# Residual stream with channels on the partitions, and 128-row scores with queries fetched from DRAM, in a two-layer decoder trunk

## Chip, cores and metric

The kernel runs on one core of a Trainium2 chip. Time is device time of one launch, in microseconds. Several executions of each kernel are timed; one more is profiled, and all rows below come from that one.

## What is computed

Two decoder layers on x of 512 tokens by 1024 channels, all in float32. Each layer is an RMS norm, one input projection split into parts, two attention branches with gates, an output projection added to x, and then a per-layer embedding (PLE). Cut to what matters here:

```python
for i in range(2):
    h = rms_norm(x, norm_gain[i])
    y = even_layer(h) if i == 0 else odd_layer(h)     # @ w_in, attention, gates, @ w_out
    x = x + y
    gate = sigmoid(rms_norm(x, ple_norm_gain[i]) @ w_ple_gate[i])
    x = x + (p[i] @ w_ple_proj[i]) * gate
# odd layer: C (8 heads, dilated keys) and D (4 heads, two softmax maps each), head size 64
s = einsum('bqhd,bshd->bhqs', q, k) * scale           # q, k: normed, rotated
```

A scores sum thus runs over 64 numbers. The kernel keeps precision by splitting each operand of a big matmul into a high and a low part in the fast float form ("fp32r"), and adding products of parts.

## The kernel before

**Data.** T = 512 tokens make NT = 4 tiles of P = 128; D = 1024 channels make NK = 8. The residual stream X is kept as two halves of the channels, X[half][:, t, :], tokens on the partitions. AT holds the normed input (without its scale) transposed: channels on the partitions, as high and low parts, `AT[:, part, k, tokens]`. `slot` is a ring of eight large SBUF buffers (L308), `raw` of four weight pieces of 128x512 and `w2` of eight split ones.

**Projections.** `proj_tok` (L406) computes tokens x columns: for each token tile t and channel block k three matmuls (high x high, high x low, low x high) with AT as the stationary operand and the weights moving, 12 matmuls for each weight piece over four tiles. Order "kt" goes through the pieces with four PSUM banks open; "tok" finishes tile after tile. `proj_gate` (L441) has the weights stationary and needs the tokens' norm scale along the free axis: `scale_rows` (L494) writes the scales to DRAM and reads them back to all partitions.

**Norms.** `norm` (L510) runs three times: before PLE of either layer, and before layer 1. For each of 4 tiles and 2 halves `turn` (L502) transposes four 128x128 blocks of X on TensorE into an `sk` bank and copies high and low parts into AT; `norm_scale` (L483) sums squares along the free axis with ScalarE and takes the power -1/2 on GpSimd. Layer 0 begins with a transposed copy of x from the host, so its input norm has no transposes.

**Scores of C and D.** `head_evac` (L571) norms, rotates and transposes queries and keys and `put_heads` (L557) stores them with 64 channels of an even head on partitions 0 to 63 and of an odd head on 64 to 127 (for D the two maps). `score_pairs` (L632) issues, for the three products of parts, a matmul on the lower 64 rows and one on the upper 64, in turn, each half with a bank of its own. Layer 0 does it differently already: `put_stacked` (L561) copies keys by DMA so that one tile holds high parts on one half of the partitions and low parts on the other, and `scores` (L624) runs two 128-row matmuls.

**Ends.** `out_half` (L729) adds the output projection to X (`add_x`, L702); `ple` (L744) evacuates with tanh of bank times the tokens' scale, two more steps on VectorE and a store.

**Order.** Nothing is issued as it is written. `Program` (L80) records every call, prices it, and `order` (L226) plays a list schedule: each engine takes the ready call with the lowest place, the place being the program's minus a lead from the table LEADS (one number for each use of a part such as "mm", "ev", "att", "w"). `issue` then emits all calls, so every instruction of the profile carries one line, L278; groups have to be read by their tiles. Each engine runs its own list strictly in order. In names, `mm` are projection banks, `sk` score banks, `tk` transpose banks, `ob` output banks.

Of the kernel before, what the change touches and what calls it, by code (L numbers as in the profile page):

```python
# [21 lines left out]
P = 128  # L22
# [9 lines left out]
    "att": (-392, -476, -265, 55, 575, -382, 44, 15, -6, -149, -341, -446, -4, -57, 63, -14, 2, 2, -287, 388, 0, 0,  # L32
# [7 lines left out]
    "idx": (-5, -2, 0),  # L40
    "mm": (15, 0, 153, 0, 10, -336, -84, 2, 8, 4, 0, -30, 30, -5, 88, -12, -304, 0, 41, 13, 136, -25, 206, -141, -135,
         -6, -996, -1930, -2303, -10383),
    "norm": (-3, -2, 0, -170, 60, -38, 0, -13, 142, 15, 0, -227, 0, -49, 15, -1, 0, 0, -396, -7, 21, 0, 0, -1844),
    "rows": (0, 898),
    "ss": (-64, 0, 0, 340, 576, 4, -39, 1269, 0, 0, -74, 119, 196, 55, 333, 112, -4, 45, -250, -182, 70, 0, 0, 1, 14,
         -119, 0, 74, 0, 1, 0, -88),
    "tab": (279, 13, -4, 0, -137, -2),
    "top": (193, -101, -908, -1349, 180, 58, -8, -21, -2, 3, -1659, -1846),
    "w": (-57, 169, 413, -21, 0, -44, -172, 0, 3, 0, -2, 1, -44, 74, -2, -20, -89, 234, 3, 68, -363, 0, 0, -80, -19,
         0, -19, 0, -854, -1336),  # L50
    "x": (2, 0),
    "y": (825, 483, 0, -2, -20, 0, 0, -16, 32, 4, 0, 202, 1, -123, -517, -335),
    None: 62,
# [4 lines left out]
SWITCH = 200  # L58
WHOLE = frozenset(range(512))
PR = 8  # L60
QB = 2
# [18 lines left out]
class Program:  # L80
# [18 lines left out]
    def __init__(self, tc):  # L99
        self.tc = tc  # L100
        for e in self.ENGINES:
            setattr(self, e, _Engine(self, e))
        self.calls, self.cost, self.after, self.rank = [], [], [], []
        self.lead, self.parts = LEADS.get(None, 0), {}
        self.touched, self.users, self.rings, self.bytes, self.groups = {}, {}, {}, {}, {}
        self.mode, self.joined, self.place, self.extra = {}, None, 0, {}
# [23 lines left out]
    def _price(self, engine, method, reads, writes):  # L130
# [22 lines left out]
        return 218 / 128 * n  # L153

    @contextmanager
    def together(self):

        self.joined = []
        yield
        i, = set(self.joined)  # L160
        self.cost[i] /= 2
        self.joined = None

    def add(self, engine, method, args, kw):
        if self.joined:
            i = self.joined[0]
            self.calls[i][1].append((method, args, kw))
        else:
            i = len(self.calls)
            self.calls.append((engine, [(method, args, kw)]))  # L170
            self.rank.append((self.place - self.lead, i))
            self.cost.append(0)
            self.after.append(set())
        self.place += 1
        if self.joined is not None:
            self.joined.append(i)
# [4 lines left out]
        if engine == "tensor":  # L181
            self.mode[i] = reads[0].ap[0][1], writes[0].ap[0][1]
# [43 lines left out]
    def order(self):  # L226
# [17 lines left out]
        dma, mode = 0.0, None  # L244
# [4 lines left out]
        while len(out) < n:  # L249
# [6 lines left out]
            if i in self.mode:  # L256
                t += SWITCH * (mode not in (None, self.mode[i]))
                mode = self.mode[i]
# [23 lines left out]
def tile_trunk(ctx: ExitStack, tc: tile.TileContext, a: dict, out: bass.AP):  # L282
# [123 lines left out]
    def proj_tok(pieces_n, evac, tiles=range(NT), order="kt", act=None, swap=0, cut=False, first=False):  # L406
# [5 lines left out]
        def mms(t, i, c0=0, c1=n, passes=range(3)):  # L412
            kt, w2 = pieces[i]
            for c in passes:
                xa, wa = PASSES[c]
                nc.tensor.matmul(banks[t][:, c0:c1], act[kt ^ (4 * swap)][:, xa, t * P:(t + 1) * P], w2[:, wa, c0:c1],
                                 start=(i == 0 and c == 0), stop=(i == last and c == 2))
        if order == "kt":
# [10 lines left out]
            for t in tiles:  # L429
                evacuate(evac, t, banks[t])  # L430
        else:
            for t in tiles:
                halves = ((0, 256), (256, 512)) if cut and t == NT - 1 else ((0, n),)
                for c0, c1 in halves:
                    banks[t] = mm_bank()
                    for i in range(last + 1):
                        mms(t, i, c0, c1)
                    evacuate(evac, t, banks[t], *((c0, c1) if cut else ()))

    @nc.part("mm")  # L440
    def proj_gate(pieces_n, y0, done, rsb):  # L441
# [3 lines left out]
        for i, (kt, w2) in enumerate(pieces):  # L445
            for m in range(4):
                for c, (xa, wa) in enumerate(PASSES):
                    nc.tensor.matmul(banks[m], w2[:, wa, m * P:(m + 1) * P], AT[:, xa, kt, :],
# [34 lines left out]
    def norm_scale(t, rs, times=1.0):  # L483
# [5 lines left out]
        if times != 1.0:  # L489
            nc.vector.tensor_scalar(out=e, in0=e, scalar1=times ** -2, scalar2=None, op0=ALU.mult)  # L490
# [11 lines left out]
    def turn(t, half, to):  # L502
        b = s_bank()
        for i in range(4):
            nc.tensor.transpose(b[:, i * P:(i + 1) * P], X[half][:, t, i * P:(i + 1) * P], ident)
        hs = slice(to * 4, to * 4 + 4)
        bv = b.rearrange("p (k n) -> p k n", k=4)
        hilo(AT[:, 0, hs, t * P:(t + 1) * P], AT[:, 1, hs, t * P:(t + 1) * P], bv)

    def norm(times=1.0, swap=0):  # L510
        rs = sb.tile([P, NT], F32, name=uid("rsn"), tag="rsn", bufs=2)
        for t in range(NT):
            for half in range(2):
                turn(t, half, half ^ swap)
            norm_scale(t, rs, times)
        return rs
# [44 lines left out]
    def put_stacked(dst, t, bank):  # L561
# [3 lines left out]
        for j, d in enumerate(dst):  # L565
# [3 lines left out]
            nc.sync.dma_start(out=d[other].bitcast(F32), in_=lo[own].bitcast(F32))  # L569

# [61 lines left out]
    def score_pairs(qT, kT, wants):  # L632

        banks = [s_bank(), s_bank()]
        found, o = [], 0
# [4 lines left out]
        found.reverse()  # L640
# [489 lines left out]
```

## Time and profile before

| | us |
|---|---|
| three runs | 676.76 median, 676.32 to 677.66 |
| profiled execution | 677.39 |
| its span, first to last instruction | 675.6 |
| TensorE busy | 668.0 (99%), 3494 matmul instructions |
| VectorE busy | 513.7 (76%) |
| ScalarE busy | 415.4 (61%) |
| GpSimd busy | 68.7 (10%) |
| DMA | 74.23 MB, 35% of 16 engines' time |

The page's timeline of 40 slices shows TensorE at nine tenths or more in every slice but the first and the last, and VectorE there from the third slice to the thirteenth (attention of layer 0) and again around the attention of C.

A matmul's busy time runs from its start to its modelled end, and the next one starts before that end. What one costs an engine that never waits is therefore the distance between starts. In the chain of waits a run of matmuls stands with its length from the first start to the start of what follows, which gives that distance directly.

### The profile page before, as it was taken

How to read it: one execution, taken by the hardware profiler on the slowest of the kernel's cores; microseconds unless marked ns; L12 is line 12 of the kernel's file. 1: busy time of each engine (PE TensorE's matmuls, PEld its weight loads, DVE VectorE, ACT ScalarE, POOL GpSimd, SP SyncE). 2: the span in 40 equal slices, each digit the busy share in tenths (PEclk: the TensorE clock that was granted, in tenths of full speed). 3: DMA queues.
4: the chain of work that ended last, by engine and by line, in shares of the span. 5: the costliest groups of instructions: out<-in, count | busy, mean ns of one | idle time of the engine just before them, and what ended most of it. 6: DMA issues, size and time to landing. Idle time of an engine off the chain costs nothing.

```text
span 675.6 us, 10378 instructions
## 1 busy us (share of the span) xinstructions
PE 668.0 (99%) x3494; PEld 543.9 (81%) x3494; DVE 513.7 (76%) x1225; ACT 415.4 (61%) x957; POOL 68.7 (10%) x55
## 2 busy tenths in 40 slices
PE   8999999999999999999999999999999999999997
PEld 5888888888988888887778877777887777888886
DVE  6699999999999646464795298989869698655443
ACT  6765678999889725355554365766637476564341
POOL 0120132000100000000230040003031000100100
PEclk9999999999999999999999999999999999999999
DMA  9855146653131521253353322123213034132222
GB/s 333 299 144 153 63 126 168 183 148 141 48 111 49 185 79 54 71 183 101 87 156 99 94 62 79 48 63 94 86 40 97 29 114 136 48 111 63 93 79 78
DMA packets 49621, 74.23 MB, mean 110 GB/s; under 512 B 5920, under 2 KB 18592, under 8 KB 49312
## 3 DMA queue, kind: packets, MB, share of 16 engines
q1 hardware_dynamic: 49424, 73.56, 35.3%
q8 instruction: 27, 0.44, 0.3%
q14 instruction: 26, 0.21, 0.1%
q10 hardware_dynamic: 144, 0.02, 0.0%
HBM read 61.49 MB, written 6.30 MB: 100 GB/s over the span
## 4 chain that ended last, share of the span: by engine, by line
PE 92%; DMA 3%; DVE 2%; ACT 1%; issue 1%; SPq 0%; DVEq 0%; ACTq 0%
PE mm L278 70%; PE sk L278 8%; PE ob L278 7%; PE tk L278 6%; DMA raw<-in_w_in_odd_dram 2%; DMA slot<-in_xT_dram 1%; DVE t L278 1%; DMA raw<-in_w_out_odd_dram 1%; DVE w L278 1%; ACT w L278 0%; DVE AT L278 0%; ACT t L278 0%; DVE slot L278 0%; SPq L278 0%; DVE tiny L278 0%
## 5 line engine op out<-in xcount | busy, mean ns | idle before, releaser
L278 PE MATMUL mm<-w,AT 128*128 128x512 f32 (+2 forms) x1728 | 433.6, 397 | 1.2 <-ACT w L278 0.6
L278 PEld LDWEIGHTS mm<-w,AT 128*128 128x128 f32 x1728 | 313.4, 188 | 69.6 <-issue 1.6
L278 PE MATMUL mm<-AT,w 128*128 128x512 f32 x384 | 104.9, 404 | 0.0
L278 ACT ACTIVATE w<-raw,gains 128x512 fp32r<-128x512 f32 x96 | 67.7, 722 | 58.8 <-PE mm L278 51.5
L278 DVE SCALAR_TENSOR_TENSOR w<-raw,gains,w 128x512 fp32r<-128x512 f32 x96 | 69.9, 746 | 39.1 <-ACT w L278 38.7
L278 POOL TENSOR_TENSOR tiny<-tiny,mhalf 128x8 f32<-128x8 f32 (+1 forms) x32 | 56.9, 1780 | 351.2 <-DVE tiny L278 351.2
L278 PEld LDWEIGHTS mm<-AT,w 128*128 128x128 f32 x384 | 68.6, 189 | 12.9 <-issue 1.1
L278 ACT ACTIVATE pr<-pr,nm 128x256 f32<-128x256 f32 (+3 forms) x128 | 68.6, 539 | 11.6 <-DVE nm L278 11.3
L278 PE MATMUL sk<-slot,slot 128*128 128x256 f32 (+7 forms) x368 | 64.6, 330 | 0.0
L278 DVE TENSOR_TENSOR w<-raw,w 128x512 fp32r<-128x512 f32 x80 | 53.8, 682 | 14.0 <-ACT w L278 13.6
L278 ACT CAST w<-raw 128x512 fp32r<-128x512 f32 x79 | 47.6, 620 | 22.2 <-PE mm L278 13.4
L278 PEld LDWEIGHTS sk<-slot,slot 64*128 64x128 f32 (+1 forms) x368 | 43.9, 187 | 12.0 <-issue 3.8
L278 PE MATMUL tk<-ident,pr 128*128 128x128 f32 x256 | 43.7, 275 | 0.0
L278 DVE SCALAR_TENSOR_TENSOR t<-t,slot 128x512 f32<-128x512 f32 (+1 forms) x17 | 11.2, 659 | 35.0 <-ACT t L278 35.0
L278 PEld LDWEIGHTS ob<-pt,Ve 128*128 128x128 f32 x272 | 35.1, 191 | 2.7 <-ACT pt L278 1.2
L278 PE MATMUL ob<-pt,Ve 128*128 128x128 f32 x272 | 37.2, 276 | 0.0
L278 PEld LDWEIGHTS tk<-ident,pr 128*128 128x128 f32 x256 | 31.2, 141 | 7.0 <-ACT pt L278 1.5
L278 ACT ACTIVATE t<-mm,rsn 128x512 f32<-128x512 f32 (+1 forms) x17 | 11.0, 662 | 40.0 <-PE mm L278 40.0
L278 DVE TENSOR_TENSOR t<-raww,tab 128x512 f32<-128x512 f32 x48 | 32.4, 684 | 4.0 <-ACT raww L278 3.9
L278 DVE CUSTOM_DVE_ANT_0 pr<-sk,cpack 128x128 f32<-128x128 f32 (+3 forms) x72 | 31.1, 461 | 5.6 <-PE sk L278 5.5
L278 ACT COPY pt<-tk 128x512 f32<-128x512 f32 (+3 forms) x56 | 27.4, 489 | 12.1 <-PE tk L278 8.6
L278 POOL TENSOR_TENSOR rsn<-tiny,mhalf 128x1 f32<-128x1 f32 x16 | 11.3, 710 | 215.6 <-DVE tiny L278 215.5
(100 smaller groups left out, 797.1 us busy)
## 6 DMA issues: line engine op xcount, KB each, us to landing
raw<-in_w_in_odd_dram SPq DMA_DIRECT2D x64, 256.0 KB, 2.8
raw<-in_w_in_even_dram SPq DMA_DIRECT2D x36, 256.0 KB, 3.0
raw<-in_w_ple_gate_dram SPq DMA_DIRECT2D x32, 256.0 KB, 2.6
slot<-in_x_dram SPq DMA_DIRECT2D x16, 256.0 KB, 6.6
raw<-in_w_out_even_dram SPq DMA_DIRECT2D x16, 256.0 KB, 2.8
raw<-in_w_out_odd_dram SPq DMA_DIRECT2D x16, 256.0 KB, 2.6
slot<-qh SPq DMA_DIRECT2D x22, 128.0 KB, 2.4
slot<-ql SPq DMA_DIRECT2D x22, 128.0 KB, 2.5
```

The lines of the kernel that those rows point to most:

```text
L278: getattr(getattr(nc, engine), method)(*args, **kw)
```

## The change

X is kept with channels on the partitions throughout: X[c][:, t, :] is now channel block 4c + t with all 512 tokens. The projections that write X (`out_half`, `ple`, `ple_products`) are flipped: weights stationary, AT moving. A norm needs no transposes: `split_x` copies a block's high and low parts into AT, `add_squares` sums squares over blocks, `column_scales` sums over partitions with one-column matmuls against -1/2, and `scale_rows` makes the row form by TensorE transposes and not through DRAM. PLE multiplies by that row before tanh. Input and output go through the host transposed. A third order of a projection, "mix", opens four banks for the first four pieces and then finishes tile by tile; with `swap` two neighbouring projections use the two halves of AT the other way round.

Keys of C and D are stacked as in layer 0 (`put_stacked`). Queries go to DRAM as high and low parts (`put_far`), and before each score group `fetch` brings a head pair's block of 128 queries to both halves of the partitions, into one of three SBUF homes used in turn (they held layer 0's values and index scores). A group is then four 128-row matmuls for each head pair and query block. The price of a change of matmul form is gone from the planner, and LEADS is a new table.

```diff
-    def score_pairs(qT, kT, wants):
+    def fetch(far, p, qb):
+        n = fetched[0] = fetched[0] + 1
+        q = sb.tile([P, 2, 2, P], F32R, name=uid("q"), tag=HOMES[n % len(HOMES)], bufs=1)
+        for u in range(2):
+            nc.sync.dma_start(out=q[64 * u:64 * u + 64].bitcast(F32),
+                              in_=far[qb][:, :, p, :].rearrange("c (j d) n -> d c j n", j=2))
+        return q
+
+    def score_pairs(far, kT, wants):
         banks = [s_bank(), s_bank()]
...
         for p, qb in reversed(wants):
             n = (qb + 1) * P
-            found.append((p, qb, o, n))
+            q = fetch(far, p, qb)
+            for j, bank in enumerate(banks):
+                for c in range(2):
+                    nc.tensor.matmul(bank[:, o:o + n], q[:, c, j, :], kT[j][:, p, :n], start=c == 0, stop=c == 1)
...
-        with nc.together():
-            for p, qb, o, n in found[::-1]:
-                for c, (qa, ka) in enumerate(PASSES):
-                    for j, bank in enumerate(banks):
-                        rows = slice(64 * j, 64 * j + 64)
-                        nc.tensor.matmul(bank[:, o:o + n], qT[qa][rows, p, qb * P:(qb + 1) * P],
-                                         kT[ka][rows, p, :n], start=c == 0, stop=c == 2)
+    def put_far(dst, t, bank):
+        hi, lo = [sb.tile([P, 4, P], F32R, name=uid(x), tag=x, bufs=QB) for x in ("qh", "ql")]
+        hilo(hi, lo, bank.rearrange("p (k n) -> p k n", k=4))
+        home = dram.tile([2, P, 4, P], F32, name=uid("far"), tag=uid("far"), bufs=1)
+        for c, part in enumerate((hi, lo)):
+            nc.sync.dma_start(out=home[c], in_=part.bitcast(F32))
+        dst[t] = home
...
     def scale_rows(rs):
+        b = t_bank()
+        for t in range(NT):
+            nc.tensor.transpose(b[:, t * P:(t + 1) * P], rs[:, t:t + 1].to_broadcast([P, P]), ident)
         rows = sb.tile([P, T], F32, name=uid("rows"), tag="rows", bufs=1)
-        line = dram.tile([NT, P], F32, name=uid("line"), tag=uid("line"), bufs=1)
-        nc.sync.dma_start(out=line.rearrange("t p -> p t"), in_=rs)
-        nc.sync.dma_start(out=rows, in_=line.rearrange("t p -> (t p)").partition_broadcast(P))
+        nc.scalar.copy(out=rows, in_=b)
         return rows
...
-    def turn(t, half, to):
-        b = s_bank()
-        for i in range(4):
-            nc.tensor.transpose(b[:, i * P:(i + 1) * P], X[half][:, t, i * P:(i + 1) * P], ident)
...
+    def split_x(k, to):
+        hilo(AT[:, 0, to, :], AT[:, 1, to, :], X[k // 4][:, k % 4, :])
+    def add_squares(acc, k):
+        sq = acc if k == 0 else tmp()
+        nc.scalar.activation(out=sq, in_=X[k // 4][:, k % 4, :], func=AF.Square, scale=1.0 / 32.0)
+        if k:
+            nc.vector.tensor_tensor(out=acc, in0=acc, in1=sq, op=ALU.add)
+    def column_scales(acc, times):
+        b = t_bank()
+        for t in range(NT):
+            nc.tensor.matmul(b[:, t:t + 1], acc[:, t * P:(t + 1) * P], mhalf[:, :1], start=True, stop=True)
...
     def norm(times=1.0, swap=0):
+        acc = sb.tile([P, T], F32, name=uid("qh"), tag="qh", bufs=QB)
+        for k in range(NK):
+            split_x(k, k ^ (4 * swap))
+            add_squares(acc, k)
+        rs = column_scales(acc, times)
+        return rs, scale_rows(rs)
...
+        elif order == "mix":
+            early = [t for t in tiles if not (cut and t == NT - 1)]
+            for t in early:
+                banks[t] = mm_bank()
+            for i in range(4):
+                for t in early:
+                    mms(t, i)
+            for t in early:
+                for i in range(4, last + 1):
+                    mms(t, i)
+                evacuate(evac, t, banks[t])
...
-                nc.scalar.activation(out=th, in_=bank[:, c0:c1], func=AF.Tanh, scale=rs[:, t:t + 1])
+                nc.vector.tensor_tensor(out=th, in0=bank[:, c0:c1], in1=rows[:, c0:c1], op=ALU.mult)
+                nc.scalar.activation(out=th, in_=th, func=AF.Tanh)
```

Three places show how the order moves. TensorE at the end of layer 0's output projection, where PLE's norm is taken; before (`slot_784` and `slot_785` are the halves of X, `mm_831` to `mm_833` output projection banks):

```order
L278 MATMUL mm_831<-w_829,AT 128x512 x3
L278 MATMUL sk_835<-ident,slot_784 128x128
L278 MATMUL mm_832<-w_823,AT 128x512
L278 MATMUL sk_835<-ident,slot_784 128x128
L278 MATMUL mm_832<-w_823,AT 128x512
L278 MATMUL sk_835<-ident,slot_784 128x128
L278 MATMUL mm_832<-w_823,AT 128x512
L278 MATMUL sk_835<-ident,slot_784 128x128
L278 MATMUL mm_832<-w_825,AT 128x512 x2
L278 MATMUL sk_836<-ident,slot_785 128x128
```

TensorE at PLE's first projection in the change, where the same norm ends (`qh_833` holds the squares, `rsn_843` the scales, `mm_863` to `mm_866` PLE's banks):

```order
L259 MATMUL tk_841<-mhalf,qh_833 128x1
L259 MATMUL mm_866<-AT,w_854 128x512 x2
L259 MATMUL mm_863<-AT,w_856 128x512 x3
L259 MATMUL mm_863<-AT,w_858 128x512 x3
L259 MATMUL mm_863<-AT,w_860 128x512 x3
L259 MATMUL mm_863<-AT,w_862 128x512 x3
L259 MATMUL tk_844<-ident,rsn_843 128x128 x3
L259 MATMUL mm_864<-AT,w_856 128x512
L259 MATMUL tk_844<-ident,rsn_843 128x128
L259 MATMUL mm_864<-AT,w_856 128x512 x2
```

The transposes of X between the output projection's matmuls are gone; PLE's first bank is finished before the four transposes of the scales stand in PE's list.

TensorE at the first score group of C; before (`slot_941`, `slot_942` are the keys' parts, `slot_1038`, `slot_1039` the queries'; six rows of 128 columns for the other query block follow):

```order
L278 MATMUL mm_1153<-AT,w_1083 128x512
L278 MATMUL sk_1095<-slot_941,slot_1038 128x256
L278 MATMUL sk_1096<-slot_941,slot_1038 128x256
L278 MATMUL sk_1095<-slot_942,slot_1038 128x256
L278 MATMUL sk_1096<-slot_942,slot_1038 128x256
L278 MATMUL sk_1095<-slot_941,slot_1039 128x256
L278 MATMUL sk_1096<-slot_941,slot_1039 128x256
```

The same engine in the change, from the third query block of the first pair to the first of the second (ahead of these rows stand the matmuls of query 1089 and two projection matmuls):

```order
L259 MATMUL mm_1245<-w_1172,AT 128x512 x2
L259 MATMUL sk_1092<-slot_916,q_1094 128x384 x2
L259 MATMUL sk_1093<-slot_917,q_1094 128x384 x2
L259 MATMUL mm_1151<-AT,w_1082 128x512
L259 MATMUL mm_1245<-w_1172,AT 128x512
L259 MATMUL mm_1152<-AT,w_1082 128x512
L259 MATMUL sk_1097<-slot_916,q_1099 128x512 x2
L259 MATMUL sk_1098<-slot_917,q_1099 128x512 x2
L259 MATMUL mm_1246<-w_1172,AT 128x512
L259 MATMUL mm_1152<-AT,w_1082 128x512
L259 MATMUL mm_1246<-w_1172,AT 128x512
L259 MATMUL sk_1119<-slot_916,q_1121 128x256 x2
```

A group is four matmuls of full height, and groups stand closer. Query 1121 takes the home of query 1089.

SyncE's queue (SP), which issues nearly all DMAs, over the same stretch in the change (`far` are the queries in DRAM, `q` the fetched blocks, `raw` weight pieces):

```order
L259 DMA far_1033<-ql_1032 128x512
L259 DMA raw_1293<-in_w_in_odd_dram 128x512
L259 DMA q_1089<-far_1033 64x4x128 x2
L259 DMA q_1121<-far_1044 64x4x128 x2
L259 DMA q_1122<-far_1033 64x4x128 x2
L259 DMA q_1127<-far_1055 64x4x128 x2
L259 DMA q_1132<-far_1066 64x4x128 x2
L259 DMA q_1221<-far_1055 64x4x128 x2
L259 DMA q_1215<-far_1044 64x4x128 x2
L259 DMA raw_1295<-in_w_in_odd_dram 128x512
```

Fetches now stand between the weight loads of the next projections. Over the whole program SP has 399 DMA issues and had 291; PE's list has 3198 matmuls and had 3330 (a plain-float one of them becomes two instructions in the profile).

## Rows read from the trace of the kernel before

**Rows 1.** Page, part 1: engine, busy us, share, instructions.
```profile
PE 668.0 (99%) x3494; PEld 543.9 (81%) x3494; DVE 513.7 (76%) x1225; ACT 415.4 (61%) x957; POOL 68.7 (10%) x55
```

**Rows 2.** Page, part 4: the chain that ended last, by engine.
```profile
PE 92%; DMA 3%; DVE 2%; ACT 1%; issue 1%; SPq 0%; DVEq 0%; ACTq 0%
```

**Rows 3.** Page, part 2: granted TensorE clock in 40 slices.
```profile
PEclk9999999999999999999999999999999999999999
```

**Rows 4.** The chain in order of time: start us, length us, what, count.
```profile
121.94 0.40 PE sk L278 x4
...
146.81 0.48 PE sk L278 x4
...
162.45 0.35 PE sk L278 x2
...
217.01 0.93 PE sk L278 x4
...
232.23 0.89 PE ob L278 x8
...
234.25 23.09 PE mm L278 x99
...
313.62 4.45 DMA raw<-in_w_in_odd_dram
...
337.21 8.31 DMA raw<-in_w_in_odd_dram
...
611.05 0.44 PE sk L278 x4
```

**Rows 5.** The same chain, score groups of C and D.
```profile
457.19 0.84 PE sk L278 x12
...
517.68 0.82 PE sk L278 x12
...
521.75 0.91 PE sk L278 x10
...
557.34 0.73 PE sk L278 x5
558.07 2.76 PE mm L278 x11
560.83 0.89 PE sk L278 x6
```

**Rows 6.** Windows: stretch, length, busy of PE, PEld, DVE, ACT, POOL, clock, DMA, GB/s.
```profile
302.00:324.00 22.00, 21.82 (x102) 17.18 (x100) 11.50 (x20) 11.91 (x23) 2.53 (x3) 1.00 0.42 126
324.00:346.00 22.00, 22.00 (x106) 17.77 (x105) 16.22 (x31) 11.13 (x21) 6.90 (x4) 1.00 0.31 81
...
395.00:440.00 45.00, 45.00 (x251) 33.96 (x250) 41.29 (x111) 29.40 (x73) 4.62 (x2) 1.00 0.21 64
```

**Rows 7.** Groups by shape: the transposes of X (busy us, mean ns, idle before).
```profile
L278 PE MATMUL sk<-ident,slot 128*128 128x128 f32 x96 | 17.8, 272 | 0.2 <-DVE AT L278 0.2
```

**Rows 8.** Timeline, the last 4.5 us: start us, length us, engine, operation.
```profile
671.38 0.47 ACT L278 ACTIVATE t<-mm,rsn 128x256 f32<-128x256 f32 x1 [2.25 <-PE mm L278]
671.89 0.43 DVE L278 SCALAR_TENSOR_TENSOR t<-t,slot 128x256 f32<-128x256 f32 x1 [1.83 <-ACT t L278]
672.35 0.42 DVE L278 SCALAR_TENSOR_TENSOR slot<-t,slot 128x256 f32<-128x256 f32 x1
```

**Rows 9.** Tile qh: issues on SP (ns min/median/max), and time to landing.
```profile
L278 SPq DMA_DIRECT2D slot<-qh x22: 590/604/805, 33.2 to 185.7; - x22
...
DMA to landing us min/median/max: 2.4/2.4/6.1
```

**Rows 10.** Groups by shape: two products on VectorE (busy us, mean ns, idle before).
```profile
L278 DVE TENSOR_TENSOR t<-mm,rows 128x512 f32<-128x512 f32 x16 | 11.0, 685 | 4.6 <-PE mm L278 4.6
...
L278 DVE TENSOR_TENSOR t<-t,t 128x256 f32<-128x256 f32 x4 | 1.7, 413 | 0.0
```

More of the change, by code (lines that the diff above doesn't have):

```diff
@@ L2 @@
 import math
-from contextlib import ExitStack, contextmanager
+from contextlib import ExitStack
 from functools import wraps
@@ L105, in __init__ @@
         self.touched, self.users, self.rings, self.bytes, self.groups = {}, {}, {}, {}, {}
-        self.mode, self.joined, self.place, self.extra = {}, None, 0, {}
+        self.place, self.extra = 0, {}
     @staticmethod
@@ L152, in _price @@
             return max(109, 0.456 * n)
[L153 to L162, printed above, removed]
-    def add(self, engine, method, args, kw):
[L165 to L173, printed above, removed]
+        return 218 / 128 * max(n, P)
+    def add(self, engine, method, args, kw):
+        i = len(self.calls)
+        self.calls.append((engine, [(method, args, kw)]))
+        self.rank.append((self.place - self.lead, i))
+        self.cost.append(0)
+        self.after.append(set())
         self.place += 1
-        if self.joined is not None:
-            self.joined.append(i)
         aps = [(k, x) for k, x in list(enumerate(args)) + list(kw.items()) if isinstance(x, bass.AP)]
@@ L243, in order @@
         earliest = [0.0] * n
-        dma, mode = 0.0, None
+        dma = 0.0
         for i in range(n):
@@ L405, in proj_tok @@
     @nc.part("mm")
-    def proj_tok(pieces_n, evac, tiles=range(NT), order="kt", act=None, swap=0, cut=False, first=False):
+    def proj_tok(pieces_n, evac, tiles=range(NT), order="kt", act=None, swap=0, cut=False, first=False, flip=False):
         pieces, n = pieces_n
@@ L415, in mms @@
                 xa, wa = PASSES[c]
-                nc.tensor.matmul(banks[t][:, c0:c1], act[kt ^ (4 * swap)][:, xa, t * P:(t + 1) * P], w2[:, wa, c0:c1],
-                                 start=(i == 0 and c == 0), stop=(i == last and c == 2))
+                x2, mine = act[kt ^ (4 * swap)], slice(t * P, (t + 1) * P)
+                if flip:
+                    nc.tensor.matmul(banks[t][:, c0:c1], w2[:, wa, mine], x2[:, xa, c0:c1],
+                                     start=(i == 0 and c == 0), stop=(i == last and c == 2))
+                else:
+                    nc.tensor.matmul(banks[t][:, c0:c1], x2[:, xa, mine], w2[:, wa, c0:c1],
+                                     start=(i == 0 and c == 0), stop=(i == last and c == 2))
         if order == "kt":
@@ L430, in proj_tok, with proj_gate @@
                 evacuate(evac, t, banks[t])
+        elif order == "mix":
[9 more added lines that the diff above has]
+                evacuate(evac, t, banks[t])
+            if cut:
+                for c0, c1 in ((0, 256), (256, 512)):
+                    banks[NT - 1] = mm_bank()
+                    for i in range(last + 1):
+                        mms(NT - 1, i, c0, c1)
+                    evacuate(evac, NT - 1, banks[NT - 1], c0, c1)
         else:
             for t in tiles:
[L433 to L438, printed above, removed]
+                banks[t] = mm_bank()
+                for i in range(last + 1):
+                    mms(t, i)
+                evacuate(evac, t, banks[t])
     @nc.part("mm")
-    def proj_gate(pieces_n, y0, done, rsb):
+    def proj_gate(pieces_n, y0, done, rsb, swap=0):
         pieces, n = pieces_n
@@ new lines, in add_squares @@
+    @nc.part("ss")
+    def add_squares(acc, k):
[3 more added lines that the diff above has]
+            nc.vector.tensor_tensor(out=acc, in0=acc, in1=sq, op=ALU.add)
+    @nc.part("rs")
+    def column_scales(acc, times):
+        b = t_bank()
+        for t in range(NT):
+            nc.tensor.matmul(b[:, t:t + 1], acc[:, t * P:(t + 1) * P], mhalf[:, :1], start=True, stop=True)
+        e = tiny(4)
+        nc.vector.tensor_scalar(out=e, in0=b[:, :NT], scalar1=-2.0 * times ** -2, scalar2=EPS * times ** -2,
+                                op0=ALU.mult, op1=ALU.add)
+        rs = sb.tile([P, NT], F32, name=uid("rsn"), tag="rsn", bufs=2)
+        nc.gpsimd.tensor_tensor(out=rs, in0=e, in1=mhalf[:, :NT], op=ALU.pow)
+        return rs
@@ L742, in reload_x, with ple @@
         load_x(range(NT), src)
-    def ple(layer, pws, rs, last, swap):
+    def ple(layer, pws, rows, last, swap):
         for c in range(2):
@@ L758, in evac @@
                 nc.vector.scalar_tensor_tensor(out=xs, in0=th, scalar=0.5, in1=xs, op0=ALU.mult, op1=ALU.add)
-                nc.sync.dma_start(out=out[0, t * P:(t + 1) * P, c * 512 + c0:c * 512 + c1] if last else xkept[c][:, t, :], in_=xs)
-            proj_tok(w, evac, order="tok", swap=swap, cut=last and c == 1)
+                k = 4 * c + t
+                nc.sync.dma_start(out=out[k * P:(k + 1) * P, c0:c1] if last else xkept[c][:, t, :], in_=xs)
+            proj_tok(w, evac, order="mix", swap=swap, cut=last and c == 1, flip=True)
     def causal(qb):
@@ L950, in tile_trunk @@
     ckT = heads()
-    proj_tok(weights(ocols("ck"), range(NK), 2), head_evac(ckT, (tab_ck[:, 0], tab_ck[:, 1]), rs1), order="tok")
+    proj_tok(weights(ocols("ck"), range(NK), 2), head_evac(ckT, (tab_ck[:, 0], tab_ck[:, 1]), rs1, put=put_stacked), order="mix", swap=1)
     rs1h = const.tile([P, NT], F32, name="rs1h")
```

102 lines of the change are left out of this document (45 added, 57 removed), and 13 rows, old and new, of the table LEADS.

## The prediction

> **What bounds the kernel now.** I read the page's busy shares first: TensorE (PE) is busy 668.0 of 675.6 us, VectorE (DVE) 513.7 [rows 1]. A busy PE need not be the bound, so the chain of work that ended last comes next: 92% of it is PE, 3% DMA, 2% DVE [rows 2]. Busy times of pipelined matmuls overlap; what one costs is the step from its start to the next one's. The same chain, in order of time, gives those steps for stretches of one kind [rows 4]: 99 projection matmuls in 23.09 us (0.233 each), four X transposes in 0.44 (0.11), four plain-float 128-column matmuls in 0.89 (eight instructions of 0.11, two for each), and for 128-row score matmuls 0.233 at 512 columns, 0.175 at 384, 0.12 at 256, 0.10 at 128. The granted clock stands at nine tenths or more of full speed in every slice [rows 3]. So each PE step taken away is worth its step, as long as DVE, ScalarE and the DMAs keep PE fed. In the two stretches around the layers' border, where the change acts first, DVE works 11.5 and 16.2 of 22 us, in the attention of C 41.3 of 45 [rows 6].
>
> **The change, part by part.** The sum is made against the profiled execution: 677.39 us, a span of 675.6 and 1.79 around it. The median of the three runs is 676.76, 0.63 lower.
>
> *Transposes of X.* Three norms times 8 turns times 4 is 96 [rows 7], gone from PE: 96 x 0.11 = **-10.6**. They stand among matmuls, and a matmul after a lone transpose starts later by as much (the group's mean of 272 ns is a duration, and four take 0.44). The copies to high and low parts stay, now out of SBUF.
> The Trainium skill (TensorE: Matmul & The Clock Gate, Part 4: PE-mode transpose) gives about 275 ns for a transpose in one kernel. The trace agrees for the duration and not for the step; by that figure as a cost, an estimate, 26.4 us would go and the sum would come to 651.
>
> *Scores of C and D.* Before, 24 groups of 64-row matmuls in pairs. Their own times in the chain (whose counts leave out some of a pair) [rows 5]: 0.84 for a group of 256 and 128 columns (4 of them), 0.82 for two of 128 (2), 0.91 for two of 256 (2), 0.73 for 384 (8), 0.89 for 512 (8): 3.4 + 1.6 + 1.8 + 5.8 + 7.1 = 19.8. Around a group the neighbours pay too: the 11 projection matmuls between two groups take 2.76 instead of 11 x 0.233 = 2.56 [rows 5], 0.195 for one change out of the 64-row form and one back; 24 x 0.195 = 4.7. After, 128 full-height matmuls, 32 of each width: 32 x (0.233 + 0.175 + 0.12 + 0.10) = 20.1, and no change of form. 20.1 - 24.5 = **-4.4**.
>
> *What PE gets.* 16 transposes of the scales in place of two trips through DRAM: **+1.8**. 12 plain-float matmuls of one column: no row has that width. From below nothing, if they hide; from above 0.22 each, the 128-column row [rows 4]. I take the upper end, since their 128-column weights are loaded either way: **+2.7**. The flipped projections have as many matmuls of the same 512 columns: 0.
>
> *The end.* After the last matmul ScalarE's tanh (0.47) and two DVE steps (0.43, 0.42) run before the store [rows 8]. Now a DVE product over 128x256 comes first, 0.413 by the nearest product of that size [rows 10], with a hand-over: **+0.45**.
>
> Sum: -10.6 - 4.4 + 1.8 + 2.7 + 0.45 = **-10.05**: span 665.5, profiled execution 667.3, median **666.7**.
>
> *Taken at nothing, with its cover.* DVE gets 21 additions of squares and 17 products of PLE (two of them half wide), some 26 us at 0.685 [rows 10], and loses some 4 us of small operations: 514 becomes 536 of 665 us. All of it falls in the three borders, where DVE has 6 to 10 us free in 22 [rows 6]. The new first half of a projection ("mix": four weight pieces for four tiles, 48 x 0.233 = 11.2 us) covers the last tile's evacuation: four steps of 0.7 and two copies, some 4.5 us. If that cover fails, PE waits for AT, then for the row of scales: 2 to 6 us over three borders, my upper bound here.
>
> SP issues 399 DMAs instead of 291: 64 fetches, 32 more half-copies of keys, 16 stores of queries, 4 fewer of others. At 0.604 us for one of 64 short runs per 64 partitions [rows 9] that is some 65 us of a queue that mostly waits. A fetch waits for its home (three tiles in turn) until the scores of the fetch that had it before are done, and the weight loads behind it in SP's queue wait too; raw has four buffers and w2 eight, 12 matmuls or 2.8 us for each piece. From the release of a home to the landing of the next query: 0.60 for the first half's issue, then 2.4 for a landing of the like shape [rows 9], 3.0 us. PE's order shows what stands between: for query 1121 ten projection matmuls, four of 384 and four of 512 columns, 2.33 + 0.70 + 0.93 = 3.96 us. Eight of the 32 fetches have less than 5 us, the least 3.7. So 0.7 us of slack at the worst: 0, with the risk below.
>
> **Rivals.**
> *Queries come late (slower).* The landing of the like copies goes up to 6.1 us [rows 9]. At that, the eight tight fetches are each some 3 us late: +24, **691 us**. For it: they share the rings with 256 KB weight pieces, and seven fetches stand in a row on SP. Against: the median is the minimum, 2.4, and the first of the row have long slack. It turns the sign when the eight are late by 10.05 / 8 = 1.25 us on average.
>
> *The border waits take the transposes' place (smaller gain).* PE fills its time at the border with transposes; without them it could come to the same weights and copies sooner and wait. The chain does hold weight loads of 4.45 and 8.31 us there [rows 4], but PE is busy 21.8 and 22.0 of 22 us [rows 6] and DVE is not full. If 6 us return: **672.7**.
>
> *Packed scores were cheap (the score edit loses).* If pairs of 64 rows took only a full matmul's step and the rest of each group were a wait that stays, the old scores cost 8 x 3 x 0.628 = 15.1 and the edit adds 5.0 instead of saving 4.4: **676.1**, no change. Against it: groups of 512 take 0.89 and not 3 x 0.233 = 0.70, in every group alike, whichever neighbour they have.
> The Trainium skill (TensorEngine Tiling (Array Packing), Performance Considerations and Theoretical Speedup) says to tile rows where the contraction is 64 or less, for up to twofold speed; that rule speaks against this change. The trace shows less than twofold: 0.149 for one of a pair against 0.233. The same page (Key Properties) says that a change of mode drains the engine; the 0.195 us agree.
>
> **How the numbers follow.** Forecast 0.83; late queries 0.06; border waits of the full size 0.08; packed scores 0.03. Low end: the column matmuls free (-2.7) and some 2 us of waits of the old schedule gone: 662. High end: the border's 6 us, or late queries at a quarter of their price: 673. About 0.2% (1.35 us) is what a measurement here can tell from no change. Late queries need 8.7 us to reach "same" and 11.4 for "slower", so of their 0.06 most is slower; packed scores are "same": faster 0.91, same 0.04, slower 0.05.
>
> **What would show it.** Right: no X transposes and no 64-row matmuls; 128-row score groups of four at 0.93 for 512 columns with neighbours at 0.233; PE still over 97% busy; some 15 us of PE steps gone and 4 to 5 new. Wrong: PE idle before score matmuls with a query's DMA as releaser; PE idle at the start of the projections after a norm with DVE's AT copy or the scale row as releaser; DVE over 90% at the borders; projection matmuls at more than 0.233 with the weights swapped in side.

## The result, and the profile after

The change runs in 666.59 us (median of 4 runs, 666.18 to 668.12); the kernel before, beside it on the same chip, in 676.54 (676.32 to 677.66). The ratio is 0.9854, 95% interval [0.9834, 0.9873], so the change is faster by 10 us. The forecast was 666.7. The profiled execution took 666.34 with a span of 664.6.

The page of the change, part 1 and two lines of part 4, against [rows 1, 2]:

```profile
PE 656.3 (99%) x3374; PEld 544.0 (82%) x3374; DVE 530.4 (80%) x1246; ACT 415.4 (63%) x937; POOL 62.2 (9%) x46
...
PE 82%; DVE 10%; DMA 5%; issue 1%; ACT 1%; SPq 1%; ACTq 0%
```

PE is still at 99% and has 11.7 us less to do; DVE has 16.7 more. The larger part of DVE in the chain is no bound: in that stretch PE waits for next to nothing. That is what the table of PE's waits shows (what PE waited for: us in all, times, the longest):

```profile
PE ob L259 <- DVE zeros L259: 1.2, 1, 1.2
PE sk L259 <- DMA q<-far: 1.0, 2, 0.7
PE tk L259 <- DVE ql L259: 0.4, 1, 0.4
PE mm L259 <- DVE w L259: 0.3, 1, 0.3
```

The first line is the start, which the kernel before has too. The second is new: two of the 32 query fetches come late, by 1.0 us together. Nothing waits for AT or for the rows of scales.

The same three windows as in [rows 6] (columns as there):

```profile
302.00:324.00 22.00, 22.00 (x101) 18.07 (x100) 18.43 (x30) 11.78 (x20) 1.01 (x1) 1.00 0.38 123
324.00:346.00 22.00, 22.00 (x101) 17.59 (x100) 11.29 (x22) 8.74 (x14) 5.66 (x3) 1.00 0.29 90
395.00:440.00 45.00, 43.98 (x220) 35.02 (x218) 35.26 (x91) 25.73 (x61) 2.61 (x1) 1.00 0.58 174
```

At the layers' border PE is busy throughout, as before. In the attention of C it idles 1.0 of 45 us, the two fetches, and the DMA share has gone from 0.21 to 0.58.

Pieces of the chain in order of time (start, length, what, count), to be held against [rows 4, 5]:

```profile
233.62 43.28 PE mm L259 x189
...
282.37 38.87 PE mm L259 x169
321.24 0.79 PE tk L259 x8
...
399.82 2.31 PE mm L259 x10
...
415.64 0.72 PE sk L259 x4
...
509.53 0.84 PE sk L259 x8
...
556.80 0.94 PE sk L259 x4
557.74 1.39 PE mm L259 x6
```

169 projection matmuls run in 38.87 us without a transpose of X between them: 0.230 each. The 189 from 233.62 on, all with AT moving, take 0.229 each; the 99 of [rows 4], with the weights moving, took 0.233. The eight `tk` instructions at 321.24 are four one-column matmuls: 0.10 for an instruction, 0.20 for a matmul. The other eight one-column matmuls stand alone, each between two projection matmuls that start 0.45 apart in the trace (at 276.87, 277.33, 277.78 for instance) and not 0.23: 0.22 for each.

A score group of 512 columns takes 0.94 (at 556.80), one of 384 takes 0.72, eight matmuls of 128 columns take 0.84 (at 509.53). The projection matmuls right behind groups, at 399.82 and 557.74, stand at 0.231 and 0.232 at once: nothing is paid for a change of form.

The fetches, by tile (issues on SP: ns min/median/max; then landing):

```profile
L259 SPq DMA_DIRECT2D q<-far x64: 573/586/971, 394.0 to 553.7; - x64
...
DMA to landing us min/median/max: 2.7/3.0/4.8
```

An issue costs what the copy of [rows 9] let expect; the median landing takes 3.0 us and not 2.4.

The end (timeline; start, length, engine, operation), against [rows 8]:

```profile
659.64 0.42 DVE L259 TENSOR_TENSOR t<-mm,rows 128x256 f32<-128x256 f32 x1 [1.03 <-PE mm L259]
660.09 0.42 ACT L259 ACTIVATE t<-t 128x256 f32<-128x256 f32 x1 [2.40 <-DVE t L259]
660.54 0.43 DVE L259 SCALAR_TENSOR_TENSOR t<-t,slot 128x256 f32<-128x256 f32 x1 [0.48 <-ACT t L259]
661.00 0.42 DVE L259 SCALAR_TENSOR_TENSOR slot<-t,slot 128x256 f32<-128x256 f32 x1
```

The product and its hand-over take 0.45 (659.64 to 660.09), as forecast; the tanh behind them takes 0.42 where it took 0.47. From the end of the last DVE step to the end of the span it is 3.2 us (661.42 to 664.6), and 2.8 before (672.77 to 675.6): the store landed later.

### The profile page after: what moved, and what is told of

Its sections match the earlier page's. It is cut to its first block, busy times and chain, and to the rows that moved or that the text cites. A ratio compares the mean times of both kernels' runs of the same rounds, so it can differ in the third digit from the quotient of the medians.

```text
span 664.6 us, 10362 instructions
## 1 busy us (share of the span) xinstructions
PE 656.3 (99%) x3374; PEld 544.0 (82%) x3374; DVE 530.4 (80%) x1246; ACT 415.4 (63%) x937; POOL 62.2 (9%) x46
## 4 chain that ended last, share of the span: by engine, by line
PE 82%; DVE 10%; DMA 5%; issue 1%; ACT 1%; SPq 1%; ACTq 0%
PE mm L259 65%; PE ob L259 6%; PE sk L259 6%; PE tk L259 5%; DVE t L259 3%; DVE pr L259 3%; DMA raw<-in_w_in_odd_dram 2%; DMA q<-far 1%; DVE w L259 1%; DVE pt L259 1%; DMA slot<-in_xT_dram 1%; DVE slot L259 1%; DVE tiny L259 1%; DVE ql L259 1%; SPq L259 1%
## 5 line engine op out<-in xcount | busy, mean ns | idle before, releaser
L259 PE MATMUL mm<-AT,w 128*128 128x512 f32 (+1 forms) x1176 | 291.1, 393 | 0.1
L259 PEld LDWEIGHTS mm<-AT,w 128*128 128x128 f32 x1176 | 212.5, 188 | 40.8 <-ACT AT L259 0.5
L259 PE MATMUL mm<-w,AT 128*128 128x512 f32 (+1 forms) x936 | 239.2, 399 | 0.4 <-DVE w L259 0.3
L259 PEld LDWEIGHTS mm<-w,AT 128*128 128x128 f32 x936 | 170.7, 189 | 35.3 <-DVE w L259 1.2
L259 POOL TENSOR_TENSOR tiny<-tiny,mhalf 128x8 f32<-128x8 f32 (+1 forms) x32 | 55.2, 1727 | 320.2 <-DVE tiny L259 282.1
L259 PE MATMUL sk<-slot,slot 128*128 128x256 f32 (+3 forms) x176 | 41.2, 322 | 0.0
L259 ACT ACTIVATE t<-t 128x512 f32<-128x512 f32 (+1 forms) x33 | 20.2, 616 | 31.2 <-DVE t L259 31.2
L259 DVE TENSOR_TENSOR t<-mm,rows 128x512 f32<-128x512 f32 (+1 forms) x33 | 22.1, 671 | 14.8 <-PE mm L259 10.0
L259 PEld LDWEIGHTS sk<-slot,slot 128*128 128x128 f32 x176 | 28.8, 189 | 4.7 <-ACT t L259 0.8
L259 DVE TENSOR_TENSOR AT<-slot,AT 128x512 fp32r<-128x512 f32 x40 | 26.9, 686 | 5.3 <-PE mm L259 3.1
```

The source lines that it names most:

```text
L259: getattr(getattr(nc, engine), method)(*args, **kw)
```

## Experiments

The theory is the prediction's: each part is worth its PE steps, since PE runs without waits. What could stand in its place: the gain is the new table of leads and not the two edits; the transposes of X were partly hidden; 64-row pairs were cheap; the slack of the fetches or of DVE is not what made the sum come out.

### The two parts in kernels without leads

`LEADS = {}` leaves every engine to the program's own order. Four kernels: before, before with the score part (score_pairs, put_far, fetch, put_stacked for keys, the three homes), before with the norm part (everything else), and the change.

```diff
-LEADS = {
-    ...
-}
+LEADS = {}
```

> The kernel before with an empty table of leads: same instructions, calls in the order of the program as far as they are ready. Theory (what PE issues sets the time, the table only keeps it fed): PE's steps stay as they were, so nothing can be gained; time rises above 676.5 by the waits that appear, with no row to size them, 0 to 40 us. It is the base for the three other runs without a table. Rival (the change's gain lies in its new table): this run and the changed kernel without a table come within 1.4 us of one another.

> Before with the score part of the change alone (stacked keys, fetched queries, 128-row matmuls), no table. Theory: 4.4 us under the base without a table, less what late queries cost there. Rival (packed pairs were cheap): 5 us over it.

> The changed kernel with the scores of before (64-row pairs, queries in SBUF), no table. Theory: 10.6 of transposes less 1.8, 2.7 and 0.45: 5.65 us under the base without a table. Rival (border waits take the transposes' place): 0 to 2 us under it.

> The changed kernel with an empty table. Theory: both parts add, 10 us under the base without a table. Rival (the gain lies in the table): within 1.4 us of it.

| without leads | us (median, range) | against before without leads |
|---|---|---|
| before | 725.68 (723.15 to 726.96) | |
| score part | 719.96 (718.04 to 721.41) | -5.7 |
| norm part | 711.39 (710.44 to 712.18) | -14.3 |
| both | 705.04 (704.31 to 707.01) | -20.6 |

Both parts gain without any table, and nearly add: 5.7 + 14.3 = 20.0. So the gain needs no table. These four kernels wait more and run in part at the lower level of PE's clock (their mean granted clock is 0.97 to 0.99, that of the two kernels with their tables 1.00), so a difference between them holds waits and clock as well as steps. The score part gives 5.7 and 6.35 (711.39 - 705.04), near its 4.4. The norm part gives much more than its 5.65 (10.6 less 1.8, 2.7 and 0.45). PE on the pages of the kernel before without leads, span 721.4 us, and of the one with the norm part, span 709.4:

```profile
PE 682.2 (95%) x3494; PEld 549.0 (76%) x3494; DVE 515.9 (72%) x1225; ACT 417.7 (58%) x957; POOL 69.5 (10%) x55
```

```profile
PE 673.5 (95%) x3438; PEld 546.4 (77%) x3438; DVE 534.9 (75%) x1246; ACT 415.2 (59%) x937; POOL 66.1 (9%) x46
```

PE idles 39.2 us in the one and 35.9 in the other: waits give 3.3 of the 12.0 us between the two spans, and PE's busy time the other 8.7. Some 2.6 of what the forecast lacks here are the flipped projections (see the part on the prediction); the rest I could not place.

### The score part under the table of before

```diff
-    cqT = heads()
-    proj_tok(wcq, head_evac(cqT, (tab_cq[:, 0], tab_cq[:, 1]), rs1))
+    cqT = {}
+    proj_tok(wcq, head_evac(cqT, (tab_cq[:, 0], tab_cq[:, 1]), rs1, put=put_far))
...
```

> Before with the score part alone, and the table of before. Theory: 20.1 us of 128-row steps for 24.5 of pairs and changes of form: 4.4 us off 676.5, 672.1, and up to 3 us more than that where the old table brings a fetch too late. Rival (packed pairs were cheap): 681.5. Rival (late queries): PE waits with the query's DMA as releaser, over 676.5.

Measured: 682.78 us (681.36 to 684.96), ratio 1.0091 [1.0072, 1.011], slower by 6.3. PE's waits:

```profile
PE sk L279 <- DMA q<-far: 3.3, 4, 1.5
PE mm L279 <- ACT raww L279: 2.6, 1, 2.6
...
PE sk L279 <- DMA far<-qh: 0.7, 1, 0.7
PE sk L279 <- DMA slot<-ql: 0.3, 1, 0.3
```

These are 6.9 us of waits, 4.3 of them on DMAs of queries and keys, and one of 2.6 before a projection matmul. That one costs beyond its length (timeline):

```profile
348.21 4.23 PE L279 MATMUL mm<-w,AT 128*128 128x512 f32 x11 [2.60 <-ACT raww L279]
```

The 11 projection matmuls behind it start 4.06 us before what follows (at 352.27), 1.5 more than 11 x 0.233. In the window from 348 to 350 the granted clock is 0.50 (1.2 GHz; 1.00 is 2.4), after PE had been idle from 346 to 348. The kernel before has 2.0 us of waits of its own behind the start, so 4.9 are new; with the 1.5, and the 4.4 saved, that makes +2.0. The two profiled executions lie 4.0 apart (681.36 and 677.39) and the medians 6.3: the rest I could not place. The prediction's first rival is thus a real mechanism: the edit alone, in an order not made for its fetches, loses.

### The norm part under a table of its own

To see the score part's worth in a suited order, the norm part alone got a table searched in the same manner as the other two.

```diff
-    cqT = {}
-    proj_tok(wcq, head_evac(cqT, (tab_cq[:, 0], tab_cq[:, 1]), rs1, put=put_far), swap=1)
+    cqT = heads()
+    proj_tok(wcq, head_evac(cqT, (tab_cq[:, 0], tab_cq[:, 1]), rs1), swap=1)
...
-LEADS = {
+LEADS = {
...
```

> The kernel before with the norm part alone, and a table of leads searched for this program in the same manner as the tables of the two kernels, so that its order is suited to it. Theory (each part is worth its steps on PE, in an order made for it): the change without its score part, 666.6 + 4.4 to 6.35 (forecast, and what the score part gave on top of the norm part in empty tables) = 671.0 to 673.0. Rival 1 (all of the tuned gain is the norm part, the score part only breaks even against its fetches): 666 to 667.5. Rival 2 (the search is worse than that of the given tables, or the norm part gains less in a suited order): 675 or more. Score groups should again stand at 0.73 for 384 columns and 0.89 for 512, with neighbours that pay.

Measured: 669.68 us (669.2 to 670.71, 5 runs), ratio 0.9899 [0.9884, 0.9913]. It fell between the theory and the first rival. The norm part gives 6.7 of the 10 us (forecast 5.65), the score part the other 3.1 (forecast 4.4). The chain shows the old groups unchanged there, with neighbours that pay:

```profile
549.49 0.89 PE sk L280 x4
550.38 2.95 PE mm L280 x12
```

12 matmuls in 2.95 us are 0.15 more than 12 x 0.233. With the 1.0 us that two fetches cost in the change, 4.4 becomes 3.4, near the 3.1. That the norm part gives 1.0 more than its forecast is no surprise once the flipped projections are counted (some 2.6 us, see the part on the prediction); that it is not 2.6 more stays open. The orders were searched apart, and how far two searched orders of one program lie from each other was not measured.

### Transposes issued twice

```diff
-        for i in range(4):
+        for i in (0, 1, 2, 3) * 2:
```

> Before with every transpose of X issued twice into the same place: 96 more of 0.11 us. Theory: 10.6 us more, 687.1. Rival (transposes fill time in which PE would wait): 0 to 5 us more. If one cost its duration of 272 ns: 26 us more.

Measured: 689.02 us (688.46 to 691.35), ratio 1.0189 [1.0169, 1.021]: 12.5 more. The group and a piece of the chain where 13 stand in a row:

```profile
L278 PE MATMUL sk<-ident,slot 128*128 128x128 f32 x192 | 30.6, 272 | 1.5 <-DVE AT L278 1.5
```

```profile
269.24 1.42 PE sk L278 x13
```

1.42 / 13 = 0.109 for one, though each is 272 ns long. 96 more are 10.5 us; two new waits of PE, 1.7 for a half of X and 1.5 for AT, more than cover the rest. So the steps were on the path in full, at 0.11 and not at their duration, for which 26 us would have been added.

### Score pairs listed apart, and half of one side left out

First the three matmuls on the lower rows are listed before the three on the upper:

```diff
-                for c, (qa, ka) in enumerate(PASSES):
-                    for j, bank in enumerate(banks):
+                for j, bank in enumerate(banks):
+                    for c, (qa, ka) in enumerate(PASSES):
```

> Before with each score group's matmuls in another order: three on the lower 64 rows, then three on the upper, instead of in turn. Theory (two halves in turn overlap, 0.149 each for 512 columns, and a lone half takes a full step): 8 x 6 x 0.628 = 30.1 for 19.8 us, 10 us more, 686.8. Rival (what a group costs has nothing to do with pairing): no change.

Measured: 676.79 us (675.29 to 678.68, 10 runs), ratio 1.0 [0.9988, 1.0012]: no change, where 10 us were expected. One group of 512 columns shows why (windows over the score matmuls alone: stretch, length, busy with the number that run in it, clock, DMA):

```profile
560.46:560.59 0.13, 0.03 (x2) 1.00 0.00 0
560.59:560.88 0.29, 0.29 (x2) 1.00 0.31 99
560.88:560.91 0.03, 0.03 (x3) 1.00 0.53 205
560.91:561.11 0.20, 0.20 (x4) 1.00 0.46 174
561.11:561.14 0.03, 0.03 (x2) 1.00 0.37 137
561.14:561.42 0.28, 0.28 (x4) 1.00 1.48 168
```

Two start together before 560.59 (at 560.56), a second pair at 560.90 and 560.91 while the first still runs, a third at 561.14. The two of a pair start 10 ns apart by the trace, where the kernel before has 3 to 4: so the list did change, and matmuls still run in pairs although three of one half are listed ahead of the other. (The trace doesn't say which half a record belongs to.) Over the groups of 512 columns in the kernel before, the steps from pair to pair are about 0.335 and 0.233: after the first, a pair follows a pair at the step of one full matmul.

So I took work off one half only: the upper rows issue the first of their three matmuls, in the same order of the program (the planner still counts the price of six). Left out are the products high x low and low x high of the odd heads of C and the second maps of D.

```diff
...
                     for j, bank in enumerate(banks):
                         rows = slice(64 * j, 64 * j + 64)
+                        if j and c:
+                            nc.place += 1
+                            continue
...
-                                         kT[ka][rows, p, :n], start=c == 0, stop=c == 2)
+                                         kT[ka][rows, p, :n], start=c == 0, stop=c == 2 or j == 1)
```

> The kernel before, with the upper half's matmuls of a score group cut to the first of three (high by high); the lower half still issues three; order unchanged. Left out: the products high x low and low x high for the odd heads of C and for the second maps of D, two of six matmuls of each group. Theory after the run with unpaired halves (the halves run beside each other, whatever the list's order, so the lower half's three steps set a group): 676.5, within 1 us. Rival (every 64-row matmul costs 0.149, as the prediction wrote): two thirds of the upper ones fewer, 24 groups' 19.8 us become some 13.2: 670.

Measured: 676.32 us (674.99 to 678.56, 12 runs), ratio 0.9999 [0.9987, 1.0011]: no change. A third of the group's matmuls is gone and the group is as long (timeline of one of 512 columns and of the matmuls behind it):

```profile
558.89 0.96 PE L278 MATMUL sk<-slot,slot 64*128 64x512 f32 x4
559.77 1.43 PE L278 MATMUL mm<-w,AT 128*128 128x512 f32 x5
```

From 558.89 to 559.77 it is 0.88; a group of that width took 0.89 with six [rows 5]. Three steps of the fuller half set it.

Together this gives the old scores another reading than the prediction's. Within a group of 512 columns the starts stand 0.335, 0.233 and about 0.32 apart (0.89 less 0.57): 3 x 0.233 = 0.70, and 0.10 for the first pair's coming in and 0.09 for going out. Outside, the neighbours pay 0.195. So a group costs its pairs at the price of full matmuls, 15.1 us over the kernel, and 0.39 for its form, 24 x 0.39 = 9.4. The sum is the prediction's 24.5.

### Homes for the queries

```diff
-HOMES = ("ve", "acc12", "acc3")
+HOMES = ("ve", "acc12", "acc3")[:1]
```

and the same with `[:2]`.

> The changed kernel with one home for queries instead of three: a fetch can't start until the scores just before it are done. Theory (slack of the three homes hides 3.0 us of landing and 0.6 of issue): the 16 fetches of C need 16 x 4.3 = 69 us where they now stand in 50, so up to 19 us more there and 0 to 8 in D; 676 in the middle, PE waiting for q's DMA. Rival (a fetch is hidden anyway, whatever the homes): 666.6.

> The change with two homes for the fetched queries in place of three. Theory: a fetch needs some 3.6 us from the release of its home (issue 0.6, landing 3.0), and with two homes only one group and the projection matmuls beside it stand between; with one home the 32 fetches cost 28.8 us, 0.9 each, and every home more takes about one group (0.9) and its neighbours off it, so most of the waits should be gone: 668 to 674. Rival 1 (two homes are as good as three, the third gives nothing): 666 to 667.5. Rival 2 (waits stay as with one): 680 or more.

One home: 695.38 us (692.6 to 698.48), ratio 1.0292 [1.0265, 1.032]. Two: 670.02 (669.91 to 670.78), 0.9905 [0.989, 0.9921]. Against the change that is 28.8 and 3.4 us. PE's waits with one home, in its longest lines:

```profile
PE sk L259 <- DMA q<-far: 4.7, 8, 1.3
PE tk L259 <- DVE t L259: 4.4, 2, 4.2
PE ob L259 <- ACT pt L259: 1.8, 4, 0.7
```

and with two:

```profile
PE ob L259 <- ACT pt L259: 3.0, 4, 1.0
PE sk L259 <- DMA q<-far: 1.9, 4, 0.8
```

Scores that come late show up behind them, as waits for the softmax's products (`pt`), and not only as waits for the fetch. With one home they also cost clock (page, busy times and granted clock in 40 slices; the span is 690.8):

```profile
PE 668.6 (97%) x3374; PEld 550.1 (80%) x3374; DVE 534.3 (77%) x1246; ACT 416.6 (60%) x937; POOL 62.4 (9%) x46
PEclk9999999999999999999999999999999989979999
```

PE idles 22.2 us (8.3 in the change), and the same 3374 instructions keep it busy 12.3 us longer. Two slices stand at 0.8 and 0.7 of the clock, and the window from 560 to 570 us at 0.66: in the trace PE is busy 16.7 us at a granted clock of 0.50, twice what the same work would take at 1.00. So some 8 of the 12.3 us, an estimate, are work at the lower level, and not all of the 28.8 is waiting.

The order is planned anew for each number of homes, so these are times of whole kernels. I had put one home at 676 in the middle; three are enough with 1.0 us left, two nearly so.

### DVE's cover at the norms

Each of the 21 additions of squares is issued twice; the second result is written over the square and not read, so nothing of the output changes (the expectation says that the scales are off, which is wrong).

```diff
             nc.vector.tensor_tensor(out=acc, in0=acc, in1=sq, op=ALU.add)
+            nc.vector.tensor_tensor(out=sq, in0=acc, in1=sq, op=ALU.add)
+            nc.place -= 1
```

> The change with each of the 21 additions of squares on DVE issued twice (14.4 us more of DVE's time at 0.685, in the stretches around the three norms); the norm's scales are off by it. Theory (DVE's extra work at the borders is covered by PE's backlog of projection matmuls): 666.6 to 668. Rival (DVE is at its limit there, PE waits for the copies of AT and the row of scales): three norms times 4.8 us, half or more of it on the path: 674 to 681.

Measured: 666.79 us (666.26 to 667.85), ratio 0.9857 [0.9841, 0.9873]: no change from the change's own 0.9854. DVE's busy time went from 530.4 to 543.3. The window of PLE's first norm in this kernel:

```profile
258.00:280.00 22.00, 22.00 (x101) 18.07 (x100) 21.91 (x36) 12.32 (x22) 0.00 (x0) 1.00 0.33 95
```

DVE is busy 21.91 of 22 us (16.83 in the change) and PE misses nothing. The cover is wider than the prediction claimed.

## Why the prediction was right, point by point

**The transposes of X: right.** They are gone, and doubling them in the kernel before costs 12.5 us with two waits, 10.5 of it steps.

**The scores: right in sum of steps, the working was off in one step and the waits cost some of it.** "The trace shows less than twofold: 0.149 for one of a pair against 0.233" is the step that failed. It divided the group's 0.89 by six. The windows show pairs that follow at 0.233, so one of a pair costs 0.117, and the rest of the group is the price of its form: 0.39 for a group and not 0.195. As the sum was taken from whole groups and their neighbours, 24.5 against 20.1 stood all the same. Here the prediction spoke against the Trainium skill with too little: TensorEngine Tiling (Array Packing), Theoretical Speedup, gives up to twofold for a contraction of 64. By the trace the steps reach it (0.233 for two). The same page of the Trainium skill says that a change of mode drains the engine (Key Properties). The 0.39 us around a group of three pairs agree. In the Trainium skill, TensorE: Matmul & The Clock Gate (the table under "Why this matters for your kernels") says that matmuls on separate rows run concurrently, started within 4 ns. The trace of the kernel before agrees, with 3 to 4 ns in most pairs; with the halves listed apart it is 10.

The rival "packed scores were cheap" was therefore half right: pairs did take a full matmul's step. It failed in its second half, "the rest of each group were a wait that stays": those 9.4 us went with the form, which turns its +5.0 into the -4.4.

**What PE gets: +1.8 right, +2.7 right.** Of the one-column matmuls four in a row take 0.20 each and the eight that stand alone 0.22: 8 x 0.22 + 0.8 = 2.6; the upper end was the one to take.

**The flipped projections at 0: wrong.** "The flipped projections have as many matmuls of the same 512 columns: 0" counts matmuls and takes their step as the same. By shape, the matmuls of 512 columns with AT moving are 384 in the kernel before and 1128 in the change:

```profile
L278 PE MATMUL mm<-AT,w 128*128 128x512 f32 x384 | 104.9, 404 | 0.0
```

```profile
L259 PE MATMUL mm<-AT,w 128*128 128x512 f32 x1128 | 285.5, 398 | 0.1
```

By the trace the mean step from one of a kind to the next is 0.2332 with the weights moving, in both kernels, and with AT moving 0.2305 in the kernel before and 0.2297 in the change. 744 x 0.0035 is some 2.6 us that the sum left out, an estimate. Why the one form is quicker no run shows.

**The end: +0.45 right for the product.** From the start of the first of the evacuating steps to the end of the last it is 1.78 us and was 1.39, so 0.39 more. The store landed 0.4 later, which nothing in the change explains.

**DVE at nothing: right.** It got 16.7 us more in all, not 22, and 12.9 us on top of that still cost nothing.

**Fetches at nothing: nearly.** Landings take 3.0 us and not the 2.4 of the copy between SBUF tiles, and 1.0 us of waits remains. The rival of late queries has the mechanism right: under the table of before the same edit costs 6.3 us, with 4.3 of waits on DMAs, and with one home 28.8. It failed here in the order of the change, which was searched with the fetches in it; that this is why is what the run under the old table suggests.

**Against which time the sum stands.** The forecast scaled from a profiled execution that was 0.85 above its median (677.39 against 676.54). Its first load of x landed late:

```profile
2.59 6.19 DMA slot<-in_xT_dram
```

That row is of the kernel before; in the change it is the next one, and the runs of the old program with altered score groups show 5.28 and 5.07.

```profile
2.59 5.30 DMA slot<-in_xT_dram
```

So 0.9 of the 11.05 us between the two profiled executions is that load, and 10.15 are left, against the forecast's 10.05. That is closer than its terms deserve, and to be met within a tenth is luck: the norm part gave 1.0 more, the score part 1.3 less than written (669.68 as the point between them). With the 2.6 us of the flipped projections the steps alone come to some -12.7; the 1.0 us of late queries and the 0.4 at the store, both at nothing in the sum, give back part of it; some 1.1 are not placed.

## What to carry to other kernels

Read the cost of packed half-height matmuls from starts inside a group, and of the group from its neighbours: the steps can be twofold cheap while the way into and out of the form, 0.39 us here, decides for groups of three pairs. Read the step of both forms of a matmul, weights moving and activations moving, before putting a swap at nothing: 0.0035 us on 744 matmuls was a quarter of this sum. Where an edit trades an engine's steps for DMAs with a few buffers, price the order with it: the same edit was worth -3.1 us in an order made for it, -5.7 and -6.35 in the program's own, and +6.3 in one made for another kernel. Parts that add over kernels without any tuning (5.7 + 14.3 against 20.6) are a cheap sign that a gain is not the tuning's, but no price of a part: there they hold waits and clock too.

## What the runs showed that I had not expected

Listing the lower half's three matmuls ahead of the upper half's changed nothing (1.0 [0.9988, 1.0012]), and dropping two of the upper three changed nothing either (0.9999 [0.9987, 1.0011]).

A wait of PE can cost beyond its length. In the kernel before without leads TensorE idles after 132 us for DVE, and the work behind it runs at the lower level of its clock (windows; columns as in [rows 6]):

```profile
130.00:134.00 4.00, 1.82 (x8) 1.09 (x8) 4.00 (x10) 2.95 (x9) 0.00 (x0) 1.00 0.58 135
134.00:138.00 4.00, 0.00 (x0) 0.00 (x0) 4.00 (x10) 0.00 (x0) 0.00 (x0) 0.88 0.51 119
138.00:142.00 4.00, 1.09 (x4) 0.71 (x4) 3.79 (x12) 0.59 (x1) 1.94 (x1) 0.50 0.22 52
...
630.00:636.00 6.00, 1.08 (x4) 0.71 (x4) 2.89 (x7) 1.92 (x4) 1.01 (x1) 0.66 0.01 3
636.00:642.00 6.00, 5.21 (x12) 4.13 (x13) 1.23 (x3) 2.20 (x5) 0.00 (x0) 0.50 0.00 0
642.00:648.00 6.00, 6.00 (x27) 4.85 (x26) 2.48 (x4) 4.74 (x8) 0.00 (x0) 0.98 0.13 44
```

A granted clock of 0.50 is 1.2 GHz, 1.00 is 2.4. From 636 to 642 us PE is busy 5.21 us with 12 matmuls, after a stretch in which it was busy 1.08 of 6; at the full clock, from 642 on, 6.00 us hold 27. Neither the change nor the kernel before with its table shows a slice below nine tenths, so none of this is in their 10 us. It is in the runs that starve PE: the score part under the old table and the change with one home, above.
